# Two token parts in one 512-column matmul, added up afterwards, and other planned costs, in a two-block transformer kernel

## The chip, the cores and the metric

The kernel runs on one core of a Trainium2 chip. Its time is device microseconds, the median of 3 runs: 2299.26 us before (2298.84 to 2300.55). All times in this document are microseconds unless they are marked ns. Engine names are those of the profile: PE is TensorE's matmuls and PEld its weight loads, DVE is VectorE, ACT ScalarE, POOL GpSimd, SP SyncE, which issues most DMAs.

## What is computed

Two transformer blocks run one after the other on 256 tokens of width 2048, in float32. The part that the change touches is the end of the first block:

```python
mix = jnp.concatenate([a_out, b_out], axis=-1) @ w_out[l]       # 2048 x 2048
x = x + gt1 * mix
h2 = rms_norm(x, g_norm2[l]) * (1 + sc2) + sh2
ffn = (jax.nn.silu(h2 @ w_gate[l]) * (h2 @ w_up[l])) @ w_down[l]  # 2048 -> 5632 -> 2048
x = x + gt2 * ffn
```

Ahead of it come the modulation (`c_act @ w_ada`, which gives gt1, sc2, sh2, gt2 and others), the keys and values of a memory, the input projection, a differential attention (a_out) and a latent attention (b_out). Behind it the second block runs: an input projection with seven parts of 1024 columns and 6144 gate columns, a spatial gating branch, a state-space branch (a complex scan over the tokens), a cross-attention to the memory, gated sums of the three branches, an output projection and a norm.

## The kernel before

**Numbers in two parts.** Each float32 operand of a large matmul is split into hi (rounded to the format fp32r) and lo (what is left). A product is then three matmuls: hi weights by hi, hi weights by lo, lo weights by hi, all added in one PSUM accumulation. Activations lie transposed, 128 features of a k tile on the partitions and 256 tokens (T) as the columns; four k tiles share a unit of 1024 columns, and hi and lo have units of their own. `ws_tile` makes one output tile: it holds 128x128 blocks of the weights in the array and moves the 256 tokens past them, for 8 to 16 k tiles.

**Weights.** Halves of 512 KB (in the down projection 384 and 320 KB) come by DMA in an order that `build_items` lists. For each half ScalarE casts hi and VectorE subtracts lo (`prep_one`), some three halves ahead of their use. The modulation's weights (ada) come in the same stream; VectorE multiplies them by the condition and accumulates (`prep_ada(False)`), or TensorE does (`prep_ada(True)`), and a chunk ends with a fold on TensorE. Chunks 6 and 7 must be there before the feed-forward part starts (`until` in `ffn`).

**Order.** The instructions are put in order while the program is built, by a planner. It has one clock for each engine: `Engine` adds a planned cost for each instruction of VectorE (V), ScalarE (S) and GpSimd (P), `mm` adds one for each matmul (E). Work that follows a matmul is an event with a due time (`later`, `at`, `chain`). `tick`, called in the matmul loops (after every 8 k tiles, that is 24 matmuls, in the second block; after 4 k tiles of both gate and up in the feed-forward part; after 2 in the other tiles of the first block), runs the events that are due. `later(n, ...)` is due (n - 1) x TICK + 0.01 later, with TICK 2.6. Events that are not hot wait while a clock of V, S or P is more than LIMIT (6.0) ahead of E. `chain` runs stages one after the other, each due when the planned work of the last is done. A pair of ada pieces goes to VectorE while V is at most 4.0 ahead (ADA_LIMIT's last value); it goes to TensorE when four pieces have arrived and V is further ahead.

**The stages that the change touches.** The output projection makes 16 tiles from the differential attention (mixA, 8 k tiles each), then 16 from the latent attention (mixB); `add_gated` adds each to x with one VectorE instruction, and for mixB `split` goes on with hi, lo and the sum of squares of x. The feed-forward part runs in 4 chunks (FCH) of 11 hidden tiles (FT). For each hidden tile, gate and up are made side by side in two PSUM tiles, 16 k tiles each; `hidden` applies SiLU to the gate, multiplies by up and splits the result. The first two hidden tiles of the first chunk (`raw`) start before the norm is known and work on x itself. After the 11 hidden tiles come 16 tiles of the down projection with 11 k tiles each, again with `add_gated`.

**The second block's scan.** 32 pairs of state groups run beside the matmuls: `ssm_pair` starts a pair, and its stages turn, scan, back and out follow as a chain of which only turn is hot. The next pair comes SSM_EVERY (5) steps later, once stage back (for odd pairs out) of this one is planned. The branch's GLU matmul waits for the last pair (`until` "yg").

Of the kernel before, what the change touches and what calls it, by code (L numbers as in the profile page):

```python
# [236 lines left out]
class Half:  # L237
    def __init__(self, hi, lo):
        self.hi, self.lo = hi, lo


class Net:
# [429 lines left out]
    def xs_chunk(self, kind, n, X, nkt, done, group=2, k0=0, pre=None):  # L672

        ps = [self.ps(), self.ps()]
        for g in range(nkt // group):
# [3 lines left out]
            for j in range(group):  # L679
                k = g * group + j  # L680
                w_hi, w_lo = h.hi[:, n * j:n * (j + 1)], h.lo[:, n * j:n * (j + 1)]
                for b in range(2):
                    xh = self.kt(X[0], k0 + k)[:, P * b:P * (b + 1)]
                    xl = self.kt(X[1], k0 + k)[:, P * b:P * (b + 1)]
# [5 lines left out]
    def ws_tile(self, kind, X, sizes, off=0, ps=None):  # L690
# [14 lines left out]
        return ps[:, :T]  # L705
# [92 lines left out]
    def memory_kv(self, mem):  # L798
        nc = self.nc
        hi, lo = [], []  # L800
        for j in range(4):
            hi.append(self.u(F32R, "mh"))
            lo.append(self.u(F32R, "ml"))
            for k in range(4 * j, 4 * j + 4):
                self.hilo(self.kt(mem, k), self.kt(hi, k), self.kt(lo, k), self.par("memg", k))
# [10 lines left out]
        for m in range(8):  # L816
            ps = self.ws_tile("wk", (hi, lo), (8, 8))
# [13 lines left out]
        for c in range(2):  # L831
# [3 lines left out]
            self.xs_chunk("wv", 512, (hi, lo), 16, lambda ps, done=done: self.later(1, lambda: done(ps), True))  # L835
# [46 lines left out]
    def first_mod(self, X, half):  # L882
# [4 lines left out]
        hi, lo = self.H  # L887
        if half:
            hi[:2], lo[:2] = [None] * 2, [None] * 2
        for j in range(2):  # L890
            hi.append(self.u(F32R, "hh"))
            lo.append(self.u(F32R, "hl"))
        def pre(g):
            if g > 3:
                return
            ks = slice(T * (2 * g % 4), T * (2 * g % 4 + 2))
            u = 2 * half + g // 2
            for k in range(8 * half + 2 * g, 8 * half + 2 * g + 2):
                x = self.kt(X, k)
                nc.scalar.activation(x, x, AF.Identity, bias=self.modc(0, k), scale=self.A1[:, k:k + 1])  # L900
            nc.scalar.copy(hi[u][:, ks], X[u][:, ks])
# [1274 lines left out]
```

## Time and profile before

| what | value |
|---|---|
| median of 3 runs | 2299.26 us (2298.84 to 2300.55) |
| the profiled execution's own time | 2300.73 us |
| its span, first to last instruction | 2299.0 us |
| mean granted TensorE clock | 0.974 |
| PE busy | 2176.5 us (95%), 16384 matmuls |
| DVE busy | 1644.7 us (72%) |
| ACT busy | 995.6 us (43%) |
| POOL busy | 383.0 us (17%) |
| read from HBM | 498.10 MB, 224 GB/s over the span |

Busy time of a matmul is modelled from its start to its end, and matmuls overlap: one of 256 columns lasts some 284 ns in the profile, while the next starts earlier. So the pace is read from the starts in a timeline, or from the count of matmuls in a stretch. Stages by their first and last instructions: the front and the attentions until 446 us, the output projection from 446 to 564, the feed-forward part until 1348, the second block to the end.

### The profile page before, as it was taken

To read this page: it belongs to the slowest core of one execution; us is meant where nothing else is said; L and a number is where in the kernel's file an instruction comes from. 1 tells how busy PE (TensorE), PEld (TensorE's weight loads), DVE (VectorE), ACT (ScalarE), POOL (GpSimd) and SP (SyncE) were. 2 spreads that over 40 slices of the span, in tenths; PEclk is the share of its full clock that TensorE was granted. 3 is DMA by queue.
4 is the path that set the end of the run, shared out by engine and by line. 5 is a ranking of instruction groups with operands and counts; after the bars stand their busy time and mean duration, and the time that the engine had idled before them with its cause. 6 is when DMAs were issued, how large, how long until landed. Compare 5 with 4: busy or idle time off the path is not lost.

```text
span 2299.0 us, 41092 instructions
## 1 busy us (share of the span) xinstructions
PE 2176.5 (95%) x16384; PEld 2058.7 (90%) x16384; DVE 1644.7 (72%) x2339; ACT 995.6 (43%) x1533; POOL 383.0 (17%) x490
## 2 busy tenths in 40 slices
PE   6998898896899999999999999999899899989996
PEld 6776676696899999999999999899899899989996
DVE  7877798999884566754664565788787878765544
ACT  5454457534443333433434444443443434344442
POOL 3200325102000002954661040010000000000012
PEclk9999899898999999999999999999999999989998
DMA  9999777797795754855765585674666566545561
GB/s 380 318 343 347 286 235 246 256 346 292 256 322 152 235 179 131 262 195 176 229 233 180 165 295 182 230 247 160 205 199 204 173 199 205 189 156 179 188 213 37
DMA packets 159282, 518.65 MB, mean 226 GB/s; under 512 B 17481, under 2 KB 22473, under 8 KB 159089
## 3 DMA queue, kind: packets, MB, share of 16 engines
q1 hardware_dynamic: 150352, 498.97, 64.6%
q10 hardware_dynamic: 8736, 17.04, 2.0%
q8 instruction: 128, 2.10, 0.4%
q14 instruction: 66, 0.53, 0.1%
HBM read 498.10 MB, written 17.84 MB: 224 GB/s over the span
## 4 chain that ended last, share of the span: by engine, by line
PE 81%; DVE 10%; ACT 3%; issue 3%; DMA 2%; POOL 1%; ACTq 0%; SPq 0%; DVEq 0%; POOLq 0%
PE p L499 80%; DVE lo L210 3%; DVE ada L210 2%; ACT hi L210 2%; DVE s L210 1%; DMA raw<-in_w_ada 1%; PE p L709 1%; PE p L420 1%; POOL rt L210 1%; DVE om L210 1%; DVE yl L210 0%; DVE xl L210 0%; ACT p L210 0%; DMA raw<-in_wk 0%; DVE h L210 0%
## 5 line engine op out<-in xcount | busy, mean ns | idle before, releaser
L499 PE MATMUL p<-yh,hi 128*128 128x256 f32 x4544 | 1294.1, 285 | 9.2 <-ACT hi L210 5.3
L499 PE MATMUL p<-yl,hi 128*128 128x256 f32 x4544 | 1290.6, 284 | 12.0 <-DVE yl L210 12.0
L499 PE MATMUL p<-yh,lo 128*128 128x256 f32 x4544 | 1291.1, 284 | 4.4 <-DVE lo L210 4.3
L210 DVE TENSOR_TENSOR lo<-raw,hi 128x1024 fp32r<-128x1024 f32 (+2 forms) x740 | 883.8, 1214 | 335.5 <-ACT hi L210 329.0
L499 PEld LDWEIGHTS p<-yh,hi 128*128 128x128 f32 x4544 | 876.5, 193 | 19.5 <-issue 6.6
L499 PEld LDWEIGHTS p<-yl,hi 128*128 128x128 f32 x4544 | 876.4, 193 | 12.9 <-DVE yl L210 12.7
L499 PEld LDWEIGHTS p<-yh,lo 128*128 128x128 f32 x4544 | 876.5, 193 | 6.2 <-DVE lo L210 5.9
L210 ACT CAST hi<-raw 128x1024 fp32r<-128x1024 f32 (+2 forms) x740 | 709.2, 993 | 224.1 <-PE p L499 121.6
L210 POOL TENSOR_TENSOR acc<-acc,sq 128x256 f32<-128x256 f32 (+1 forms) x56 | 59.5, 1063 | 969.7 <-ACT sq L210 966.4
L210 DVE SCALAR_TENSOR_TENSOR ada<-raw,cact,ada 128x1024 f32<-128x1024 f32 x162 | 208.0, 1329 | 0.0
L499 PE MATMUL p<-hi,hh 128*128 128x512 f32 (+1 forms) x256 | 102.5, 401 | 8.4 <-ACT hh L210 6.6
L210 ACT ACTIVATE sg<-p 128x256 f32<-128x256 f32 x42 | 16.1, 383 | 216.9 <-PE p L499 216.9
L499 PE MATMUL p<-lo,hh 128*128 128x512 f32 (+1 forms) x256 | 101.3, 396 | 5.1 <-DVE lo L210 5.0
L210 DVE SCALAR_TENSOR_TENSOR x<-p,mod,x 128x256 f32<-128x256 f32 x96 | 46.2, 481 | 78.8 <-PE p L499 78.7
L499 PE MATMUL p<-hi,hl 128*128 128x512 f32 (+1 forms) x256 | 100.8, 394 | 0.0
L210 ACT ACTIVATE gt<-gt 128x256 f32<-128x256 f32 x48 | 20.1, 418 | 162.3 <-DVE gt L210 160.9
L210 POOL TENSOR_TENSOR rot<-tab,tab 128x256 f32<-128x256 f32 x64 | 63.9, 998 | 100.8 <-DMA dR<-rot 100.8
L499 PEld LDWEIGHTS p<-hi,hh 128*128 128x128 f32 x256 | 50.3, 197 | 22.2 <-ACT hh L210 7.0
L210 DVE TENSOR_TENSOR s<-p,rot 128x512 f32<-128x512 f32 x64 | 41.1, 685 | 36.6 <-PE p L499 36.5
L499 PEld LDWEIGHTS p<-lo,hh 128*128 128x128 f32 x256 | 50.2, 196 | 16.6 <-DVE lo L210 7.8
L210 POOL TENSOR_TENSOR rt<-rs 128x16 f32<-128x16 f32 (+2 forms) x26 | 13.5, 518 | 294.9 <-DVE rs L210 289.6
L210 POOL TENSOR_TENSOR rt<-tab,tab 128x256 f32<-128x256 f32 x64 | 62.2, 971 | 0.0
(300 smaller groups left out, 1972.4 us busy)
## 6 DMA issues: line engine op xcount, KB each, us to landing
raw<-in_w_ada SPq DMA_DIRECT2D x192, 512.0 KB
raw<-in_w_gu SPq DMA_DIRECT2D x176, 512.0 KB
raw<-in_w SPq DMA_DIRECT2D x96, 512.0 KB
raw<-in_w2g SPq DMA_DIRECT2D x96, 512.0 KB
raw<-in_w_out SPq DMA_DIRECT2D x64, 512.0 KB
raw<-in_w_in SPq DMA_DIRECT2D x56, 512.0 KB
raw<-in_w_down SPq DMA_DIRECT2D x64, 384.0 KB
raw<-in_wb SPq DMA_DIRECT2D x48, 512.0 KB
```

The source lines that it names most:

```text
L210: return f(*args, **kw)
L420: self.nc.tensor.matmul(self.ada_row[32 * j:32 * j + 32, :], left, w, start=start, stop=last)
L499: self.nc.tensor.matmul(out, lhsT, rhs, start=start, stop=stop)
L709: self.nc.tensor.transpose(out, in_, self.flip if flip else self.ident)
```

## The change

Activations now come in `Pairs`: hi and lo of a k tile lie side by side in 512 columns, two k tiles to a unit. In the output projection and in the feed-forward part (without its two early tiles) `mm_pair` runs one matmul of 512 columns with the hi weights, whose halves of the PSUM bank get the products with hi and with lo, and one of 256 columns with the lo weights into the first half. The two halves are added when they are read: `add_gated` runs twice, and `hidden` has a stage `fold` ahead of `gate`. The other stages use the new layout with the three matmuls of before. The planner's costs of VectorE, ScalarE, GpSimd and of a matmul are others.

```diff
 class Engine:
-    fixed = {"V": 0.07, "S": 0.2, "P": 0.06}
-    least = {"V": 0.2, "S": 0.23, "P": 0.28}
-    each = {"V": 0.00105, "S": 0.00074, "P": 0.00223}
+    fixed = {"V": 0.155, "S": 0.2, "P": 0.16}
+    least = {"V": 0.17, "S": 0.23, "P": 0.28}
+    each = {"V": 0.00106, "S": 0.00083, "P": 0.00223}
...
+class Pairs:
+    def __init__(self, net, name="y"):
+        self.net, self.name, self.units = net, name, []
+
+    def both(self, k):
+        while len(self.units) <= k // 2:
+            self.units.append(self.net.u(F32R, self.name))
+        return self.units[k // 2][:, 512 * (k % 2):512 * (k % 2 + 1)]
+
+    def hi(self, k):
+        return self.both(k)[:, :T]
+
+    def lo(self, k):
+        return self.both(k)[:, T:]
+
+    def two(self, k, part):
+        self.both(k)
+        return self.units[k // 2].rearrange("p (k h t) -> p k h t", k=2, h=2)[:, :, part]
...
     def mm(self, out, lhsT, rhs, start, stop):
         n = math.prod(rhs.shape[1:])
-        self.load.at["E"] += (max(n, 2 * P) if rhs.dtype == F32R else 4 * max(n, P)) / 2400
+        self.load.at["E"] += (max(n, P) + 32 if rhs.dtype == F32R else 4 * max(n, P)) / 2400
...
+    def mm_pair(self, ps, whi, wlo, X, k, start, stop, two):
+        if two:
+            self.mm(ps, whi, X.both(k), start, False)
+        else:
+            self.mm(ps[:, :T], whi, X.hi(k), start, False)
+            self.mm(ps[:, :T], whi, X.lo(k), False, False)
+        self.mm(ps[:, :T], wlo, X.hi(k), False, stop)
...
-    def ws_tile(self, kind, X, sizes, off=0, ps=None):
+    def ws_tile(self, kind, X, sizes, off=0, ps=None, two=False):
...
-                self.mm(ps[:, :T], h.hi[:, w], self.kt(X[0], off + k), k == 0, False)
-                self.mm(ps[:, :T], h.hi[:, w], self.kt(X[1], off + k), False, False)
-                self.mm(ps[:, :T], h.lo[:, w], self.kt(X[0], off + k), False, k == last)
+                self.mm_pair(ps, h.hi[:, w], h.lo[:, w], X, off + k, k == 0, k == last, two)
...
-            self.add_gated(self.ws_tile("w_out", self.mixA, (8,)), X, m, 2)
+            self.add_gated(self.ws_tile("w_out", self.mixA, (8,), two=True), X, m, 2)
...
-            self.add_gated(self.ws_tile("w_out", self.mixB, (8,)), X, m, 2, split)
+            self.add_gated(self.ws_tile("w_out", self.mixB, (8,), two=True), X, m, 2, split)
...
     def add_gated(self, ps, X, m, part, then=None):
         def add():
             x = self.kt(X, m)
-            self.nc.vector.scalar_tensor_tensor(x, ps, self.modc(part, m), x, op0=ALU.mult, op1=ALU.add)
+            for v in (ps[:, :T], ps[:, T:]):
+                self.nc.vector.scalar_tensor_tensor(x, v, self.modc(part, m), x, op0=ALU.mult, op1=ALU.add)
...
     def ffn(self):
...
                         for ps, hf in ((pg, hg), (pu, hu)):
+                            if not raw:
+                                self.mm_pair(ps, hf.hi[:, w], hf.lo[:, w], H, k, k == 0, k == 15, True)
+                                continue
...
-                self.add_gated(self.ws_tile("w_down", hid, (6, 5)), X, m, 5, split if last else None)
+                self.add_gated(self.ws_tile("w_down", hid, (6, 5), two=True), X, m, 5, split if last else None)
...
     def hidden(self, pg, pu, hid, j, raw):
+        def fold():
+            for v, ps in ((g, pg), (u, pu)):
+                nc.scalar.copy(v, ps[:, T:])
+                nc.vector.tensor_tensor(v, ps[:, :T], v, op=ALU.add)
+
         def gate():
-            if raw:
-                nc.scalar.activation(g, g, AF.Silu, bias=bias[0])
-            else:
-                nc.scalar.activation(g, pg[:, :T], AF.Silu)
+            nc.scalar.activation(g, g, AF.Silu, bias=bias[0] if raw else 0.0)
...
-                nc.vector.tensor_tensor(g, g, pu[:, :T], op=ALU.mult)
-            nc.scalar.copy(self.kt(hid[0], j), g)
+                nc.vector.tensor_tensor(g, g, u, op=ALU.mult)
+            nc.scalar.copy(hid.hi(j), g)
...
         elif j == FT - 1:
+            fold()
             gate()
             product()
             low()
         else:
-            self.chain(0, gate, product, low, hot=(gate, product, low))
+            self.chain(0, fold, gate, product, low, hot=(fold, gate, product, low))
```

Everywhere else `self.kt(X[0], k)` and `self.kt(X[1], k)` become `X.hi(k)` and `X.lo(k)`, and `grow` goes; copies of several k tiles at once (`first_mod`, `diff_norm`, the split of yg) write through `two`, with a stride of 512 columns.

## Rows read from the trace of the kernel before

**Rows 1.** The page: busy time (share of span), instructions; tenths in 40 slices.
```profile
PE 2176.5 (95%) x16384; PEld 2058.7 (90%) x16384; DVE 1644.7 (72%) x2339; ACT 995.6 (43%) x1533; POOL 383.0 (17%) x490
...
PE   6998898896899999999999999999899899989996
...
PEclk9999899898999999999999999999999999989998
```
**Rows 2.** Stretches: length, then busy us (count) by engine, granted clock, DMA share, GB/s.
```profile
446.00:500.00 54.00, 53.58 (x426) 51.50 (x427) 48.14 (x65) 24.52 (x35) 0.00 (x0) 1.00 0.91 317
500.00:564.00 64.00, 49.39 (x393) 48.53 (x391) 63.76 (x73) 22.89 (x43) 15.96 (x15) 0.91 0.87 319
613.00:1350.00 737.00, 736.53 (x6121) 735.50 (x6121) 449.93 (x622) 302.83 (x413) 219.69 (x259) 1.00 0.64 208
1410.00:2000.00 590.00, 575.72 (x4511) 553.04 (x4510) 474.07 (x748) 245.84 (x329) 5.93 (x11) 0.99 0.62 202
2000.00:2030.00 30.00, 21.44 (x140) 19.15 (x139) 21.45 (x35) 10.58 (x15) 0.00 (x0) 0.77 0.23 72
```
**Rows 3.** Timeline of PE, feed-forward part: start, duration, instruction; 15 starts apart.
```profile
1000.10 0.28 PE L499 MATMUL p<-yh,lo 128*128 128x256 f32 x1
...
1001.90 0.28 PE L499 MATMUL p<-yh,lo 128*128 128x256 f32 x1
```
**Rows 4.** Groups by form, 650 to 1400 us: busy, mean ns | idle before.
```profile
L499 PE MATMUL p<-yh,hi 128*128 128x256 f32 x2077 | 588.2, 283 | 0.0
...
L210 DVE TENSOR_TENSOR lo<-raw,hi 128x1024 fp32r<-128x1024 f32 x172 | 225.4, 1336 | 161.7 <-ACT hi L210 159.2 <-POOL cft L210 1.5 <-POOL rt L210 1.1
```
**Rows 5.** Waits of PE, 430 to 700 us: total, times, longest.
```profile
PE p L420 <- DVE ada L210: 12.0, 1, 12.0
```
**Rows 6.** Waits of PE, 1400 to 2300 us.
```profile
PE p L499 <- DVE yl L210: 12.0, 3, 6.6
PE p L499 <- DVE s L210: 6.3, 2, 4.7
PE p L499 <- ACT yh L210: 3.2, 1, 3.2
```
**Rows 7.** Timeline of PE in the second block, 512-column matmuls; 6 starts apart.
```profile
1471.16 0.39 PE L499 MATMUL p<-lo,yh 128*128 128x512 f32 x1
...
1472.52 0.39 PE L499 MATMUL p<-lo,yh 128*128 128x512 f32 x1
```
**Rows 8.** Instructions on tile mod: min/median/max ns, first and last start; here add_gated's.
```profile
L210 DVE SCALAR_TENSOR_TENSOR x<-p,mod,x x96: 471/484/486, 452.9 to 1348.2; 128x256 f32<-128x256 f32 x96
```
**Rows 9.** Timeline of DVE in the second half of the output projection.
```profile
510.01 0.47 DVE L210 SCALAR_TENSOR_TENSOR xl<-x,A,xh 128x256 fp32r<-128x256 f32 x1
510.41 0.47 DVE L210 SCALAR_TENSOR_TENSOR x<-p,mod,x 128x256 f32<-128x256 f32 x1
510.80 0.47 DVE L210 SCALAR_TENSOR_TENSOR xl<-x,A,xh 128x256 fp32r<-128x256 f32 x1
511.19 1.28 DVE L210 SCALAR_TENSOR_TENSOR ada<-raw,cact,ada 128x1024 f32<-128x1024 f32 x1
```
**Rows 10.** Instructions on tile sg of `hidden`: the gate and the product.
```profile
L210 ACT ACTIVATE sg<-p x42: 380/383/386, 620.5 to 1284.5; 128x256 f32<-128x256 f32 x42
L210 DVE TENSOR_TENSOR sg<-sg,p x42: 408/414/422, 627.3 to 1284.9; 128x256 f32<-128x256 f32 x42
```
**Rows 11.** Timeline at the last chunk's end: last gate, its lo, first down tile read.
```profile
1284.46 0.38 ACT L210 ACTIVATE sg<-p 128x256 f32<-128x256 f32 x1 [7.29 <-PE p L499]
...
1285.79 0.43 DVE L210 TENSOR_TENSOR yl<-sg,yh 128x256 fp32r<-128x256 f32 x1 [0.47 <-ACT yh L210]
...
1288.78 0.48 DVE L210 SCALAR_TENSOR_TENSOR x<-p,mod,x 128x256 f32<-128x256 f32 x1 [0.67 <-PE p L499]
```
**Rows 12.** Instructions on tile rdec: the scans, two for each of 32 pairs.
```profile
L210 DVE TENSOR_TENSOR_SCAN s<-rdec,sw x64: 664/676/689, 1440.1 to 2012.4; 128x256 f32<-128x256 f32 x64
```
**Rows 13.** Waits of PE, 0 to 430 us.
```profile
PE p L709 <- DVE km L210: 5.4, 1, 5.4
```

More of the change, by code (lines that the diff above doesn't have):

```diff
@@ L704, in ws_tile @@
                     self.tick()
-        return ps[:, :T]
+        return ps if two else ps[:, :T]
     def transpose(self, out, in_, flip=False):
@@ L886, in first_mod @@
         nc.vector.scalar_tensor_tensor(self.A1[:, ks], self.modc(1, 8 * half, 8), 1.0, self.par("g1", 8 * half, 8), op0=ALU.add, op1=ALU.mult)
-        hi, lo = self.H
+        H = self.H
         if half:
[L889 to L892, printed above, removed]
+            H.units[:4] = [None] * 4
         def pre(g):
@@ L895, in pre @@
                 return
-            ks = slice(T * (2 * g % 4), T * (2 * g % 4 + 2))
-            u = 2 * half + g // 2
-            for k in range(8 * half + 2 * g, 8 * half + 2 * g + 2):
+            k0 = 8 * half + 2 * g
+            xx = X[k0 // 4][:, T * (k0 % 4):T * (k0 % 4 + 2)].rearrange("p (k t) -> p k t", k=2)
+            for k in range(k0, k0 + 2):
                 x = self.kt(X, k)
                 nc.scalar.activation(x, x, AF.Identity, bias=self.modc(0, k), scale=self.A1[:, k:k + 1])
-            nc.scalar.copy(hi[u][:, ks], X[u][:, ks])
-            self.freer(512).tensor_tensor(lo[u][:, ks], X[u][:, ks], hi[u][:, ks].bitcast(F32), op=ALU.subtract)
+            nc.scalar.copy(H.two(k0, 0), xx)
+            self.freer(512).tensor_tensor(H.two(k0, 1), xx, H.two(k0, 0).bitcast(F32), op=ALU.subtract)
         pre(0)
@@ L908, in attention_block @@
         self.A1 = self.c([P, 16], s="A1")
-        self.H = H = ([], [])
+        self.H = H = Pairs(self, "hh")
         order = [[(ch, 0) if ch[0] == "c" else (ch[0], int(ch[1])) for ch in o] for o in ORDER]
@@ L1257, in diff_pv @@
         if h == 0:
-            self.mixA, self.otok = [[], []], []
+            self.mixA, self.otok = Pairs(self, "mixA"), []
         if h % 4 == 0:
-            self.grow(self.mixA)
             self.otok.append(self.u(s="ot"))
@@ L1428, in start_mla @@
     def start_mla(self):
-        self.mixB = [[], []]
+        self.mixB = Pairs(self, "mixB")
         self.later(MLA_AT, lambda: self.mla_next(0))
@@ L1461, in ffn @@
         nc = self.nc
-        X, H = self.X, ([], [])
+        X, H = self.X, Pairs(self, "h2")
         self.until(lambda: {6, 7} <= self.mod_done)
@@ L1472, in ffn @@
                 self.steps(self.ssm_early(), 2)
-            hid = ([], [])
+            hid = Pairs(self, "hid")
             for j in range(FT):
@@ L1747, in second @@
         yg_hl = self.yg_hl
-        Y = [[], []]
+        Y = Pairs(self, "yb")
         for m in range(8):
-            if m % 4 == 0:
-                self.grow(Y)
             ps = self.ws_tile("glu", yg_hl, (8,))
@@ L1769, in second @@
             self.chain(1, sigmoid, product, hi, lo, hot=(sigmoid, product, hi, lo))
-        M = [[], []]
-        for _ in range(4):
-            self.grow(M)
+        M = Pairs(self, "m")
         self.gate_loop(H, Y, third, "yb")
@@ L1812, in gated_tiles @@
     def gated_tiles(self, H, other, name):
-        Y = [[], []]
+        Y = Pairs(self, name)
         for m in range(8):
-            if m % 4 == 0:
-                self.grow(Y)
             self.gated(self.ws_tile("w2", H, (8, 8)), other(m), Y, m, name if m == 7 else None)
@@ L2123, in ssm_out @@
         t, bxt = self.t(s="ge")[:, :T], self.bxt
+        pair = lambda j: self.yg[j // 2][:, 512 * (j % 2):512 * (j % 2 + 1)].rearrange("p (k t) -> p k t", k=2)
         def skip():
@@ L2143, in hi @@
             self.cf = None
-            self.yg_hl = ([], [])
-            for j in range(2):
-                self.grow(self.yg_hl)
-                nc.scalar.copy(self.yg_hl[0][j], self.yg[j])
+            self.yg_hl = Pairs(self, "ygp")
+            for j in range(4):
+                nc.scalar.copy(self.yg_hl.two(2 * j, 0), pair(j))
         def lo():
-            for j in range(2):
-                self.freer(1024).tensor_tensor(self.yg_hl[1][j], self.yg[j], self.yg_hl[0][j].bitcast(F32), op=ALU.subtract)
+            for j in range(4):
+                h = self.yg_hl
+                self.freer(512).tensor_tensor(h.two(2 * j, 1), pair(j), h.two(2 * j, 0).bitcast(F32), op=ALU.subtract)
             self.ready_set.add("yg")
```

66 lines of the change are left out of this document (26 added, 40 removed).

## The prediction

> **What bounds the kernel now.** I read the page's totals and slices first, then stretches by stage, then the waits, then single instructions. TensorE is busy 95% of the span and its slices are nines nearly everywhere, with the granted clock at nine tenths or more in most [rows 1]. A busy TensorE is not yet one that sets the end, so the stretches decide [rows 2]. From 613 to 1350 us, the feed-forward part, 6121 matmuls start in 737 us: one each 120.4 ns, at a granted clock of 1.00. Single starts there lie 120 ns apart, 15 steps in 1.80 us [rows 3], and the costliest group has 0.0 us of idle time ahead of it [rows 4]. So this stage is pure matmul pace: what a matmul costs less there comes off the end. VectorE is busy 450 of those 737 us and ScalarE 303; both have room.
>
> Three other stretches are bound otherwise. From 500 to 564 us, the second half of the output projection, VectorE is busy 63.8 of 64 us [rows 2], and TensorE then stands 12.0 us for the last accumulation of the modulation (ada) [rows 5]. From 1410 to 2000 us TensorE leads again, with stalls that VectorE ends. From 2000 to 2030 only 140 matmuls start; at 120 ns they need 16.8 us, so 13.2 us go there, of which 6.3 and 3.2 us are waits for the tail of the state-space scan (s, yh) [rows 2, 6].
>
> **The change part by part.**
>
> *Pairs of matmuls become one.* Where two 256-column matmuls with the same hi weights follow each other (moving hi, then lo), one of 512 columns now runs; the third, lo weights by hi, stays. The kernel has 512-column matmuls of this kind in another place: they start 6 steps in 1.36 us apart, 227 ns [rows 7]. Two of 120 ns less one of 227 ns is 13 ns for each k tile. Their number, from the code: gate and up, 42 tiles (44 less the two early ones, which keep their form) x 16 k x 2 = 1344; down, 4 x 16 x 11 = 704; output projection, 32 x 8 = 256. The first two lie in the stretch that is pure pace: 2048 x 13 ns = 26.6 us. The 256 of the projection would give 3.3 us, but that stage ends with the wait of 12.0 us for VectorE, so I count them at nothing.
>
> The Trainium skill ("TensorE: Matmul & The Clock Gate", section "Back-to-back issue gap") speaks against this: it gives the gap as the columns over 2.4 GHz plus about 2.5 ns, so that a merged pair would save 2.5 ns alone. By that, 2048 pairs give 5.1 us (an estimate) and the sum below would be 2293. The rows differ: 120 ns against its 109 and 227 against its 216, so the fixed part here is about 13 ns, and I go by the rows.
>
> *The halves are added up afterwards.* add_gated now runs two scalar_tensor_tensors on VectorE instead of one, 96 more. One takes 484 ns [rows 8], but such instructions start 0.40 us apart when queued [rows 9]. In the down projection that is 64 x 0.40 = 25.6 us of VectorE. In the gate and up tiles fold adds, 42 times, two ScalarE copies out of PSUM (nearest row 383 ns) and two VectorE adds (nearest 414 ns) [rows 10]: 32 us of ScalarE and 35 of VectorE. With these VectorE has some 510 of 710 us and ScalarE 335; TensorE's matmuls cover all of it: nothing. Without the cover, at most the 25.6 + 35 us of VectorE would show. On the path fold could stand only at the end of a chunk, where the first down tile needs the 11th hidden tile at its last k. At 1284.46 us the last gate starts, at 1286.22 the lo part is there, and that down tile's result is read at 1288.78 [rows 11]. Its last three matmuls began some 0.5 us before that, so 2.0 us were to spare. fold puts one copy and one add ahead, 0.8 us, and 0.3 more as both engines take turns; the down tile itself is 0.13 us shorter. I take 0; if a weight cast or subtraction (1.34 us [rows 4]) stands in between at all four ends, at most 6 us.
>
> *The projection's stage on VectorE.* 32 of the additional instructions lie between 446 and 564 us. In the first 54 us VectorE has 5.9 us idle [rows 2], which takes up most of 16 x 0.40 = 6.4 us. In the second 64 us it has none, so 6.4 us come straight onto the wait that ends the stage: together +7. Against it, the build can give a pair of ada pieces to TensorE instead when its clock for VectorE is loaded, and with VectorE dearer in that clock it will do so sooner; one pair takes 2 x 1.28 us off VectorE [rows 9]. Bounds: -5 (five pairs moved) to +13 (no idle time used). I take +4, about one pair moved.
>
> *The build's clock.* Every instruction's planned cost changes, and with it the order in which the queues are filled; no instruction count follows directly. In the second part the planner looks at its events after each 24 matmuls. It charged 24 x 256 / 2400 = 2.56 us for them and now charges 24 x 288 / 2400 = 2.88, which is what they take by [rows 3]. A delay of "two steps" (2.61 us) so falls on the second look before and on the first now; the five steps between pairs of the state-space scan (10.41 us) fall on the fourth look in place of the fifth. The scans' 32 pairs now run from 1440.1 to about 2011.8 us (the pair's second scan starts at 2012.4 [rows 12]), 18.4 us or 6.4 looks each, so the chain within a pair also counts, not the delay alone. One look less would be 15.6 us a pair, half a look 17.0; anything under 18.0 moves the scan's end ahead of the place where TensorE now stands for it. The gain is bounded by 13.2 us there [rows 2] and the 12.0 us of waits for yl [rows 6]: -25. Denser scans also make VectorE fuller than 474 of 590 us, which could double those yl waits: +12. I take -5, half of the two waits on s and yh, since the planned costs of VectorE rise too. Ahead of 440 us nothing is merged; a reordered event there is worth about the longest wait of that kind, 5.4 us [rows 13], either way, and I take 0.
>
> *Layout.* hi and lo of a k tile now share a buffer; the units in use stay the same in number (6 for the hidden tiles, 8 for h2), and strided copies move the same elements: 0.
>
> **Sum**, on the profiled run's 2300.73 us (span 2299.0): -26.6 + 4 + 0 - 5 = 2273.1. The median is 1.5 us below that run, so 2272.
>
> **The rivals.**
>
> A. *The scan's tail vanishes* and the projection loses nothing: all 13.2 us at 2000 to 2030 and some of the yl waits come back. Time 2250 to 2262. For it: the delays fall on earlier looks. Against: 6.4 looks a pair say that the chain, not the delay, sets much of the pace.
>
> B. *Slower: the scan comes later.* The dearer VectorE (0.155 in place of 0.07 us fixed) makes the planner put off events that are not urgent while more than 6 us are queued, and three of the four stages of a scan pair are of that kind. TensorE already waits at the scan's end, so each 1 us more a pair is 31 us at the end. Without the 5 us of above, 22.6 us are left to outweigh, which takes 0.73 us a pair, 19.2 us in place of 18.4; at 1 us the time is 2273.1 + 5 + 31 - 1.5 = 2308. Against: the planner's TensorE is dearer too (12.5%), so VectorE's relative load rises only for short instructions.
>
> C. *The pair doesn't get cheaper.* The matmuls of [rows 7] are 512 columns after 512; alternating with 256 might keep the whole 13 ns. Bounds 0 to 13 ns a pair; at 0 the time is 2298. No row shows such an alternation at length; the weight loads beside the matmuls are the same kind, so I give it little.
>
> D. *The additions show*: projection at +13, chunk ends at +6, front +5: 2283 to 2296.
>
> **How the numbers follow.** Forecast (own range 2262 to 2283) 0.60; A 0.17; B 0.10; C 0.03; D 0.10. 0.2% of the median is 4.6 us, about what a measurement of this kernel can tell from no change, so faster is below 2294.7. Faster: 0.60 + 0.17 + 0.08 of D + 0.01 of C = 0.86; within: 0.02 of D, 0.02 of C and 0.01 of B = 0.05; slower 0.09 of B. The range 2252 to 2296 leaves out some 0.05 of A and 0.12 above.
>
> **What would show it.** In the feed-forward stretch a 512- and a 256-column matmul of one k tile should take 347 ns together in place of 360, and that stretch should be some 26 us shorter with no waits inside it; 360 would be C. Between the projection's start and the first gate tile the stage should be no shorter, with VectorE full and the wait for ada of 12 us or more. The scans' first and last start tell A and B apart: under 18.0 us a pair or over 19. A stall before each down projection would show fold on the path. The forecast is wrong if the feed-forward part's gain is there but given back behind 1400 us.

## The result, and the profile after

The changed kernel takes 2275.64 us (median of 4 runs, 2274.93 to 2277.15). The kernel before, on the same chip, takes 2299.91 (4 runs, 2298.84 to 2300.91). The ratio is 0.9895, with a 95% interval of 0.988 to 0.991. The forecast was 2272.0, 3.6 us below the result, in a range of 2252 to 2296.

The page of the changed kernel, the lines of [rows 1]: busy time and instructions by engine, then tenths in 40 slices.

```profile
PE 2150.8 (95%) x14128; PEld 1929.4 (85%) x14128; DVE 1711.9 (75%) x2510; ACT 1023.5 (45%) x1618; POOL 380.1 (17%) x490
...
PE   6998898996899999999999999999899899999996
...
PEclk9999999997999999999999999999999999999998
```

TensorE has 2256 matmuls fewer and 25.7 us less busy time, and the span is 24.9 us shorter (2274.1 against 2299.0). That the two times nearly agree is partly chance, as the stages show. Each mark below is the start of an instruction in the traces: the first matmul of the output projection, the first one on x itself (xh) in the early gate tile, the first one of the normed gate tiles, and the last addition of the down projection.

| us | projection starts | early gate (xh) | normed gate | last down addition | end |
|---|---|---|---|---|---|
| before | 446.4 | 570.6 | 599.3 | 1348.2 | 2299.0 |
| after | 426.4 | 567.7 | 594.9 | 1326.5 | 2274.1 |
| stage, before | | 124.2 | 28.7 | 748.9 | 950.8 |
| stage, after | | 141.3 | 27.2 | 731.6 | 947.6 |

The stretch ahead of the projection gives 20.0 us and the projection takes 17.1 of them back; the early tiles give 1.5, the feed-forward part 17.3 and the second block 3.2: 24.9 in all.

The stretches of the changed kernel that answer to [rows 2]: length, busy time and count by engine, granted clock, DMA share, GB/s.

```profile
426.00:480.00 54.00, 46.46 (x256) 36.70 (x255) 42.25 (x68) 19.97 (x36) 0.00 (x0) 0.97 0.74 257
480.00:540.00 60.00, 60.00 (x351) 49.69 (x350) 58.43 (x81) 26.87 (x43) 8.93 (x12) 1.00 0.85 299
540.00:564.00 24.00, 5.93 (x27) 1.89 (x26) 23.89 (x28) 5.50 (x9) 4.46 (x3) 0.60 0.99 391
613.00:1326.00 713.00, 712.95 (x4069) 621.34 (x4068) 509.04 (x762) 327.75 (x492) 224.36 (x258) 1.00 0.66 213
700.00:880.00 180.00, 180.00 (x1040) 158.72 (x1040) 133.32 (x281) 80.43 (x117) 55.12 (x78) 1.00 0.61 194
900.00:1320.00 420.00, 420.00 (x2379) 364.35 (x2378) 280.76 (x368) 193.02 (x292) 147.86 (x158) 1.00 0.65 206
1400.00:1980.00 580.00, 562.47 (x4398) 539.86 (x4398) 473.37 (x751) 241.42 (x322) 6.00 (x11) 0.99 0.64 202
1980.00:2010.00 30.00, 27.36 (x212) 26.22 (x212) 19.78 (x31) 15.15 (x23) 0.00 (x0) 0.94 0.39 129
```

The fifth and the sixth row are the reading that matters most. Both lie inside the feed-forward part, at a granted clock of 1.00 and with TensorE busy throughout, yet a k tile (two matmuls) takes 2 x 180 / 1040 = 346 ns in the one and 2 x 420 / 2379 = 353 ns in the other. The first three rows are the output projection: towards its end VectorE is nearly full (23.89 of 24 us), while TensorE is busy for only 5.93 of these 24 us, at a granted clock of 0.60. The last row shows that the hole behind the scans [rows 2, fifth row] is gone: 212 matmuls in 30 us in place of 140.

Single starts at the two paces, from the timeline of TensorE (start, duration, instruction):

```profile
800.13 0.39 PE L522 MATMUL p<-h,hi 128*128 128x512 f32 x1
800.36 0.28 PE L522 MATMUL p<-h,lo 128*128 128x256 f32 x1
800.48 0.39 PE L522 MATMUL p<-h,hi 128*128 128x512 f32 x1
...
1000.06 0.40 PE L522 MATMUL p<-h,hi 128*128 128x512 f32 x1
1000.29 0.28 PE L522 MATMUL p<-h,lo 128*128 128x256 f32 x1
1000.41 0.40 PE L522 MATMUL p<-h,hi 128*128 128x512 f32 x1
1000.64 0.28 PE L522 MATMUL p<-h,lo 128*128 128x256 f32 x1
1000.76 0.40 PE L522 MATMUL p<-h,hi 128*128 128x512 f32 x1
1001.00 0.28 PE L522 MATMUL p<-h,lo 128*128 128x256 f32 x1
1001.12 0.40 PE L522 MATMUL p<-h,hi 128*128 128x512 f32 x1
```

At 800 us the 512-column matmul holds the next one off for 230 ns each time. At 1000 us three k tiles take 350, 350 and 360 ns, 1.06 us in all, again and again. From the trace's starts the first pace is 346.7 ns a k tile (230.0 + 116.7) and the second 353.4 (236.5 + 116.9). The second begins at 893 us and holds for 1221 k tiles up to 1326 us.

What stands at the place where it begins:

```profile
893.04 0.39 PE L522 MATMUL p<-hid,hi 128*128 128x512 f32 x1
893.27 0.28 PE L522 MATMUL p<-hid,lo 128*128 128x256 f32 x1
893.60 0.50 PE L522 MATMUL p<-hid,hi 128*128 128x512 f32 x1
893.94 0.28 PE L522 MATMUL p<-hid,lo 128*128 128x256 f32 x1
```

From 893.27 the next start comes after 0.33 us in place of 0.12, and the one behind it after 0.34 in place of 0.23: the first down tile of the second chunk needs the eleventh hidden tile, whose lo part VectorE ends only at 893.54. This is the place that the forecast named for fold.

The waits of TensorE in the changed kernel, in the order 430 to 700 us, 640 to 1380 us, and 1400 us to the end (total, times, longest); they answer to [rows 5, 6]:

```profile
PE p L443 <- DVE ada L210: 18.8, 2, 18.1
PE p L522 <- ACT hi L210: 6.0, 1, 6.0
...
PE p L522 <- DVE diag L210: 2.0, 1, 2.0
PE p L522 <- POOL acc L210: 0.3, 1, 0.3
...
PE p L522 <- DVE yx L210: 6.1, 2, 5.4
PE p L522 <- DVE ya L210: 5.6, 1, 5.6
...
PE p L522 <- DVE sd L210: 2.2, 1, 2.2
...
PE p L522 <- ACT ygp L210: 2.1, 1, 2.1
```

The last of these views has no wait for s. The waits of 2.0 us for diag and of 0.3 us for acc stand at 1337 and 1329 us, behind the feed-forward part.

Fold and the additional additions run beside the matmuls, at about the durations that were taken for them. The instructions on the tiles mod, sg and rdec (count: minimum/median/maximum ns, first and last start) answer to [rows 8, 10, 12]; the last row are the scans of the second block.

```profile
L210 DVE SCALAR_TENSOR_TENSOR x<-p,mod,x x192: 470/484/489, 435.5 to 1326.5; 128x256 f32<-128x256 f32 x192
...
L210 ACT COPY sg<-p x84: 359/374/378, 616.3 to 1263.5; 128x256 f32<-128x256 f32 x84
L210 DVE TENSOR_TENSOR sg<-p,sg x84: 406/424/429, 619.8 to 1263.9; 128x256 f32<-128x256 f32 x84
...
L210 DVE TENSOR_TENSOR_SCAN s<-rdec,sw x64: 659/672/685, 1418.3 to 1980.9; 128x256 f32<-128x256 f32 x64
```

### The profile page after: what moved, and what is told of

Same layout as the page of the kernel before. It is cut to its first block, busy times and chain, and to the rows that moved or that the text cites. A ratio compares the mean times of both kernels' runs of the same rounds, so it can differ in the third digit from the quotient of the medians.

```text
span 2274.1 us, 36916 instructions
## 1 busy us (share of the span) xinstructions
PE 2150.8 (95%) x14128; PEld 1929.4 (85%) x14128; DVE 1711.9 (75%) x2510; ACT 1023.5 (45%) x1618; POOL 380.1 (17%) x490
## 4 chain that ended last, share of the span: by engine, by line
PE 72%; DVE 14%; DMA 4%; issue 3%; POOL 3%; ACT 2%; ACTq 0%; SPq 0%; DVEq 0%; POOLq 0%
PE p L522 72%; DVE lo L210 4%; DVE ada L210 3%; DVE s L210 2%; DMA raw<-in_w_ada 2%; ACT hi L210 1%; POOL tab L210 1%; POOL rt L210 1%; DVE lg L210 1%; POOL rot L210 1%; DVE om L210 1%; PE p L443 0%; POOL tabt L210 0%; DVE part L210 0%; DMA dV<-memV 0%
## 5 line engine op out<-in xcount | busy, mean ns | idle before, releaser
L522 PE MATMUL p<-h,hi 128*128 128x256 f32 (+1 forms) x4416 | 1031.2, 318 | 7.2 <-ACT hi L210 7.2
L522 PE MATMUL p<-h,lo 128*128 128x256 f32 x2880 | 812.7, 282 | 1.7 <-DVE lo L210 1.7
L522 PEld LDWEIGHTS p<-h,hi 128*128 128x128 f32 x4416 | 731.9, 191 | 74.7 <-ACT hi L210 8.6
L522 PEld LDWEIGHTS p<-h,lo 128*128 128x128 f32 x2880 | 549.5, 191 | 2.7 <-DVE lo L210 2.6
L522 PE MATMUL p<-hid,hi 128*128 128x512 f32 x704 | 247.8, 397 | 0.1
L522 PE MATMUL p<-hid,lo 128*128 128x256 f32 x704 | 197.6, 281 | 0.0
L522 PEld LDWEIGHTS p<-hid,hi 128*128 128x128 f32 x704 | 132.1, 188 | 32.3 <-DVE hid L210 0.4
L522 PEld LDWEIGHTS p<-hid,lo 128*128 128x128 f32 x704 | 133.0, 189 | 0.0
L522 PE MATMUL p<-m,hi 128*128 128x256 f32 x512 | 92.2, 283 | 0.0
L522 PEld LDWEIGHTS p<-m,hi 128*128 128x128 f32 x512 | 79.9, 192 | 0.0
```

## The experiments

Three questions were open. How is the time shared between the pairs of matmuls and the build's clock? Why does the projection give back what the stretch ahead of it gains? What sets the pace of the feed-forward stream? Ten kernels were run. Here is what each came to: the median and the ratio are those of all its runs, while the three columns behind them are read from the one execution that was profiled; "xh at" is the start of the early gate, and "stage" the feed-forward part from the normed gate to the last down addition.

| kernel | median us | ratio to before, 95% | xh at | stage | second block |
|---|---|---|---|---|---|
| after | 2275.64 | 0.9895 (0.988 to 0.991) | 567.7 | 731.6 | 947.6 |
| clock_only | 2287.61 | 0.9949 (0.9935 to 0.9964) | 560.0 | 750.1 | 948.0 |
| pairs_old_clock | 2280.24 | 0.9921 (0.9905 to 0.9938) | 579.0 | 723.8 | 948.4 |
| reset | 2277.72 | 0.9901 (0.9886 to 0.9916) | 568.2 | 730.1 | 950.0 |
| grouped | 2273.2 | 0.989 (0.9875 to 0.9904) | 566.2 | 729.1 | 947.2 |
| proj_single | 2268.43 | 0.9856 (0.9838 to 0.9873) | 559.7 | 732.8 | 946.8 |
| proj_single_grouped | 2267.37 | 0.9853 (0.9833 to 0.9872) | 561.4 | 729.6 | 946.7 |
| ada_half_dve | 2232.51, one run | | 527.9 | 729.1 | 946.6 |
| ada_half_dma | 2287.92, one run | | 577.9 | 733.9 | 946.5 |
| lo_first_one | 2270.07 | 0.9871 (0.9855 to 0.9888) | 560.2 | 733.0 | 949.1 |
| lo_first_all | 2273.67 | 0.9887 (0.9873 to 0.9902) | 559.3 | 734.4 | 948.5 |

**clock_only**: the kernel before with the changed planner's costs alone.

```diff
-    fixed = {"V": 0.07, "S": 0.2, "P": 0.06}
-    least = {"V": 0.2, "S": 0.23, "P": 0.28}
-    each = {"V": 0.00105, "S": 0.00074, "P": 0.00223}
+    fixed = {"V": 0.155, "S": 0.2, "P": 0.16}
+    least = {"V": 0.17, "S": 0.23, "P": 0.28}
+    each = {"V": 0.00106, "S": 0.00083, "P": 0.00223}
...
-        self.load.at["E"] += (max(n, 2 * P) if rhs.dtype == F32R else 4 * max(n, P)) / 2400
+        self.load.at["E"] += (max(n, P) + 32 if rhs.dtype == F32R else 4 * max(n, P)) / 2400
```

> The kernel before with the other planned costs alone (no pairs, no additions). Theory 1: the planned costs bring the first projection matmul forward by about 20 us (to 426), but the projection still ends when the ada pieces are through (the 160th piece is done at 564 us in both traces), so the first early gate tile starts at 568 +- 4 and the whole kernel gains only 3 to 7 us: 2293 to 2297. Rival 2: the 17 us that the projection lost are the 32 additional VectorE instructions; without them the early start is kept, the gate tile starts at 548 to 556 and the time is 2278 to 2286. Rival 3: the early start comes from the new layout, not from the costs: first projection matmul at 446, time 2297 to 2301.

Measured: 2287.61 us, 12 us below before, with the early gate at 560.0. Time and early gate both lie between the ranges of theory 1 and rival 2. So the new planned costs alone (the build's clock) bring the early gate 10.6 us forward.

**pairs_old_clock**: the changed kernel with those six values as before.

> The changed kernel with the planned costs of before (VectorE, ScalarE, GpSimd and matmul). Theory 1: the feed-forward part keeps its 18 to 27 us; the projection starts near 446 again and the early gate tile at 568 to 575, because the ada pieces set it; time 2274 to 2284. Rival 2: the 32 additions cost VectorE their full 12.8 us ahead of the gate tile, which starts at 580 to 585; time 2286 to 2290. In the second block the scan's pairs should take 18.4 us as before.

Measured: 2280.24 us, inside theory 1's time, with the early gate at 579.0, 8.4 us later than before and between the two ranges given. The feed-forward part shrinks by 25.1 us, close to the 26.6 of the forecast. With clock_only this gives a square: the pairs cost 8.4 us ahead of the early gate with the old costs and 7.7 with the new ones, and the new costs gain 10.6 us without the pairs and 11.3 with them. The stretches of pairs_old_clock:

```profile
700.00:880.00 180.00, 180.00 (x1041) 158.72 (x1040) 123.45 (x259) 81.04 (x119) 0.00 (x0) 1.00 0.59 191
...
900.00:1300.00 400.00, 400.00 (x2310) 352.69 (x2309) 284.96 (x362) 185.35 (x278) 214.59 (x249) 1.00 0.67 212
```

Both give 346 ns a k tile; from the starts, 1839 k tiles in a row keep 346.7 ns. The same code in the same loops thus runs nearly the whole part at the faster pace here, and 60% of it at the slower one in the changed kernel. This is the execution that was profiled, of 2278.18 us; the four runs are 2278.09, 2278.18, 2282.30 and 2282.37, and no trace shows which pace the two longer ones had.

**reset**: the changed kernel with seven transposes put into the stream, one ahead of the first gate tile of each later chunk and one ahead of the second down tile of each chunk.

```diff
+                if j == 0 and c:
+                    self.nc.tensor.transpose(pg[:, :P], self.ident, self.ident)
...
```

> The changed kernel with seven more PE transposes (of the identity, into a PSUM bank that the next matmul overwrites): ahead of the second down tile of each chunk and ahead of the first gate tile of chunks 2 to 4. In the changed kernel a k tile takes 346.7 ns until 893 us and 353.3 ns from there to 1326. Theory 1: which of the two it is, is settled by how the last interruption of the matmul stream left weight loads and matmuls to each other, and transposes leave the faster one (as at 427, 481 and 676 us); then all chunks run at 346.7, 1250 k tiles gain 6.7 ns, 8.3 us, less 7 x 0.2 us: time 2267 to 2270. Rival: the slower pace belongs to the buffers or the neighbours from chunk 2 on (GpSimd's tables, other weight buffers); then 353.3 stays and the time is 2275 to 2278.

Measured: 2277.72 us (2271.29 to 2278.41), in the rival's time, but the pace does not go by place as the rival said. From the starts: 346.7 ns behind the transposes at 712, 956, 1084 and 1141 us, 347.0 behind the one at 1267, and 353.3 behind those at 769 and 898. Behind a wait of 1.2 us at 1046 us it goes from 346.7 to 353.4. So a transpose is a place where the pace can change, but it doesn't restore the faster one; theory 1 falls in that form, and the rival with it.

**grouped**: gate's and up's 512-column matmuls first, then the two of 256 columns.

```diff
-                        for ps, hf in ((pg, hg), (pu, hu)):
-                            if not raw:
-                                self.mm_pair(ps, hf.hi[:, w], hf.lo[:, w], H, k, k == 0, k == 15, True)
-                                continue
+                        if not raw:
+                            for ps, hf in ((pg, hg), (pu, hu)):
+                                self.mm(ps, hf.hi[:, w], H.both(k), k == 0, False)
+                            for ps, hf in ((pg, hg), (pu, hu)):
+                                self.mm(ps[:, :T], hf.lo[:, w], H.hi(k), False, k == 15)
```

> The changed kernel with the order of the gate and up matmuls of one k turned from 512, 256, 512, 256 columns into 512, 512, 256, 256. Theory 1 (the slower pace belongs to the alternation after an interruption): a k of both takes 693 ns in all chunks, the 704 gate and up k tiles behind 893 us gain 6.7 ns, 4.7 us: time 2269 to 2273; the down tiles may still show 353.3. Rival: the pace belongs to the place in time: 707 ns per k of both from 893 us on, time 2275 to 2278. A third: two 512-column matmuls in a row have less cover for the weight loads, more than 707 ns: 2280 or more.

Measured: 2273.2 us, 0.2 above theory 1's range, and its interval overlaps that of the changed kernel. From the starts, the gate and up tiles of all four chunks keep one pace, 348.3 ns a k tile (696.6 for gate and up together, where theory 1 said 693, the rival 707 and the third over 707). The down tiles of the same execution, which still alternate, take 353.3 ns in the first chunk and 346.7 in the other three. So in this execution the two paces go with the alternation.

**proj_single**: the changed kernel with the output projection back to three 256-column matmuls and one addition.

```diff
-            self.add_gated(self.ws_tile("w_out", self.mixA, (8,), two=True), X, m, 2)
+            self.add_gated(self.ws_tile("w_out", self.mixA, (8,)), X, m, 2)
...
-            self.add_gated(self.ws_tile("w_out", self.mixB, (8,), two=True), X, m, 2, split)
+            self.add_gated(self.ws_tile("w_out", self.mixB, (8,)), X, m, 2, split)
...
-            for v in (ps[:, :T], ps[:, T:]):
+            for v in ((ps,) if part == 2 else (ps[:, :T], ps[:, T:])):
```

> The output projections back to three 256-column matmuls and one addition for each modulation of the second part; the feed-forward pairs and the build's clock stay. Theory 1 (the 32 more additions on a full VectorE are what the pairs cost ahead of the early gate: 7.7 us between clock_only's first early gate tile at 560.0 us and after's at 567.7): first early gate tile at 560 +-2 us, 2267 to 2270 us. Rival (the cost comes from the layout of the two halves or from where the modulation's matmuls land, not from the additions): first early gate tile at 566 to 570 us, 2274 to 2278 us.

Measured: 2268.43 us with the early gate at 559.7; theory 1 holds to the half microsecond. The stretch from the start up to the early gate, first of before, then of clock_only, of the changed kernel and of proj_single:

```profile
0.00:570.60 570.60, 496.66 (x2783) 409.02 (x2783) 481.28 (x620) 281.95 (x557) 120.43 (x194) 0.94 0.87 306
```
```profile
0.00:560.00 560.00, 491.25 (x2798) 406.20 (x2798) 485.06 (x629) 283.00 (x558) 114.53 (x184) 0.95 0.88 313
```
```profile
0.00:567.70 567.70, 492.55 (x2574) 391.90 (x2575) 490.59 (x656) 284.12 (x561) 111.75 (x184) 0.95 0.87 308
```
```profile
0.00:559.70 559.70, 488.04 (x2799) 404.02 (x2799) 485.28 (x630) 283.13 (x559) 114.31 (x184) 0.96 0.87 313
```

The third busy figure is VectorE's. Read as a ledger: the new planned costs leave VectorE 14.4 us less idle (570.6 - 481.3 = 89.3 to 560.0 - 485.1 = 74.9) and give it 3.8 us more work, so the early gate comes 10.6 us sooner. The pairs then add 5.5 us of work and 2.2 of idle time, 7.7 in all. Taking them out of the projection alone gives all of it back, though TensorE has 225 matmuls more ahead of the early gate. The edit takes out the merged matmuls and the additions together; since TensorE has more to do without the merging, the additions are the part that can cost.

**proj_single_grouped**: both edits together.

> The same edit of the output projections, with the feed-forward matmuls of gate and up in the order 512, 512, 256, 256. Theory 1: as in proj_single the first early gate tile comes at 558 to 562 us, the feed-forward part keeps the 729 us of grouped, 2262 to 2268 us. Rival (the projection's cost is not the additions): 2271 to 2276 us as grouped, first early gate tile at 565 to 569 us.

Measured: 2267.37 us, within theory 1's range, the early gate at 561.4 and the feed-forward part 729.6 us. Its interval and that of proj_single all but coincide, so the order of gate and up is worth nothing that these runs can tell. In its trace too gate and up take 348.3 ns a k tile, and the down tiles 346.7 in three chunks and 353.3 in the third. Both kernels lie below the changed one: the ends of their intervals (0.9873 and 0.9872) are under its lower end (0.988).

**ada_half_dve**: VectorE's accumulation of the modulation is left out for odd k, its planned cost and all transfers stay; so half of VectorE's part of the modulation's sum is missing.

```diff
+                elif k % 2:
+                    self.load.add("V", Engine.fixed["V"] + Engine.each["V"] * 1024)
                 else:
                     nc.vector.scalar_tensor_tensor(acc[n], w, c, acc[n], op0=ALU.mult, op1=ALU.add)
```

> VectorE's accumulation of the modulation for odd k is left out, so part of the modulation's sum is missing; the transfers stay. Theory 1 (VectorE, busy 525 of 564 us, ends the stretch up to the early gate): first early gate tile 30 us or more earlier than 567.7, at 500 to 538 us, and 2205 to 2245 us. Rival (the transfers of the modulation's weights, with a DMA share of 0.87, end it): first early gate tile at 560 to 568 us, 2267 to 2277 us.

**ada_half_dma**: only the first half of the columns of each ada piece is loaded, and used twice; VectorE works on it in two instructions of 512 columns.

```diff
-            self.nc.sync.dma_start(r[:, :n], src)
+            if isinstance(kind, tuple):
+                self.load.add("D", P * n * 4 / 358e3)
+                self.nc.sync.eng.dma_start(r[:, :512], src[:, :512])
+            else:
+                self.nc.sync.dma_start(r[:, :n], src)
...
-                    nc.vector.scalar_tensor_tensor(acc[n], w, c, acc[n], op0=ALU.mult, op1=ALU.add)
+                for o in (0, 512):
+                    y = acc[n][:, o:o + 512]
...
+                        v.scalar_tensor_tensor(y, w[:, :512], c, y, op0=ALU.mult, op1=ALU.add)
```

> Only the first half of the columns of each weight piece of the modulation is loaded and used twice, so the modulation is another one; VectorE's work stays. Theory 1 (VectorE ends the stretch up to the early gate): first early gate tile at 560 to 568 us, 2267 to 2277 us. Rival (the transfers end it): first early gate tile at 500 to 545 us, 2205 to 2255 us.

The stretch up to the early gate, first of ada_half_dve, then of ada_half_dma:

```profile
0.00:527.90 527.90, 479.07 (x2575) 384.48 (x2575) 410.76 (x590) 283.55 (x561) 102.01 (x184) 0.98 0.89 324
```
```profile
0.00:577.90 577.90, 498.54 (x2574) 396.64 (x2575) 506.85 (x792) 284.17 (x561) 104.83 (x184) 0.94 0.69 227
```

VectorE is busy 490.6 of the 567.7 us of this stretch in the changed kernel; the 525 of the expectation is a sum of durations that overlap. With 79.8 us less work on VectorE (490.6 to 410.8) the early gate comes 39.8 us sooner and the time falls to 2232.51, as theory 1 has it. With the DMA share down from 0.87 to 0.69 it comes no sooner at all: it comes 10.2 us later, beyond both ranges, and VectorE's work is 16.3 us more, because two instructions of 512 columns cost more than one of 1024. That side effect had been left out of the expectation. Both kernels, each from one run, agree that VectorE's work sets this stretch, not the transfers: of each microsecond of VectorE, half to two thirds reaches the early gate.

**lo_first_one** and **lo_first_all**: proj_single with the last k tile of a down tile turned round, its 256-column matmul first, in the first down tile of each chunk and in all down tiles. The low half of the last hidden tile is then needed later, and the wait that stands at 893 us in the changed kernel should go.

```diff
+        if two == "lo first" and stop:
+            self.mm(ps[:, :T], wlo, X.hi(k), start, False)
+            self.mm(ps, whi, X.both(k), False, True)
+            return
```

> proj_single with one change: in the first down tile of each chunk the eleventh (last) hidden tile's 256-column matmul goes ahead of its 512-column matmul, so that the low half of that hidden tile is needed some 117 ns later; the wait of about 0.1 us behind which after and proj_single went over to 353 ns for each k should go. Theory 1 (the pace of the stream is settled where it is interrupted, and this wait is the interruption): 346.7 ns for each k from about 670 us through 1300, the feed-forward part 8 us shorter than proj_single's 732.8 (724 to 726 us), 2258 to 2263 us. Rival (the pace changes there for another reason, or the swapped order interrupts the stream as well): 353 ns over half or more of the part, feed-forward part 730 to 735 us, 2265 to 2270 us.

> The same swap at the last k of all 128 down tiles, so that two 512-column matmuls follow on each other at each seam between down tiles. Theory 1 (only a wait settles the pace; a 512 behind a 512 does not): as lo_first_one, feed-forward part 724 to 727 us, 2258 to 2264 us. Rival (any change of the order settles it anew, so that both paces stand side by side by place): mean of 348 to 352 ns for each k, feed-forward part 727 to 732 us, 2262 to 2268 us.

Measured: lo_first_one 2270.07 us and lo_first_all 2273.67; nothing gained, and theory 1 falls in both. The wait did go, and the pace changed without it. The stretches of lo_first_one between its four turned tiles (at about 701, 888, 1072 and 1260 us; between the second and the third stretch stands a wait of 1.6 us):

```profile
705.00:885.00 180.00, 180.00 (x1021) 156.01 (x1020) 134.62 (x278) 78.20 (x112) 66.93 (x92) 1.00 0.60 193
890.00:1020.00 130.00, 130.00 (x752) 114.62 (x751) 97.86 (x110) 56.62 (x77) 124.61 (x129) 1.00 0.77 249
1075.00:1255.00 180.00, 180.00 (x1021) 155.98 (x1020) 105.57 (x144) 77.64 (x112) 0.00 (x0) 1.00 0.61 193
1262.00:1315.00 53.00, 53.00 (x307) 46.74 (x306) 42.69 (x71) 30.52 (x57) 9.70 (x13) 1.00 0.70 210
```

They are 353, 346, 353 and 345 ns a k tile. The first turned tile, in the timeline (x2: two matmuls drawn together):

```profile
700.68 0.39 PE L522 MATMUL p<-hid,hi 128*128 128x512 f32 x1
700.91 0.28 PE L522 MATMUL p<-hid,lo 128*128 128x256 f32 x1
701.03 0.39 PE L522 MATMUL p<-hid,hi 128*128 128x512 f32 x1
701.26 0.40 PE L522 MATMUL p<-hid,lo 128*128 128x256 f32 x2
701.50 0.63 PE L522 MATMUL p<-hid,hi 128*128 128x512 f32 x2
701.96 0.28 PE L522 MATMUL p<-hid,lo 128*128 128x256 f32 x1
```

No engine is waited for there, and ahead of it the k tiles take 346.7 ns, behind it 353. At 888 us the same turn does the reverse. In lo_first_all, with such a turn every 11 k tiles of the down projection, the faster pace holds up to the first turned k tile, at about 702 us, and hardly anywhere behind it; the mean is 352.1 ns. So lo_first_one fits the rival's broader sentence, that a change of the order settles the pace anew. In lo_first_all the two paces don't stand side by side, and its numbers lie above the rival's (348 to 352 ns, 727 to 732 us, 2262 to 2268 us): 352.1, 734.4 and 2273.67.

## Why the prediction was right, and where it was not

**Pairs in the feed-forward part: predicted -26.6, measured -17.3.** The mechanism is as forecast: the stage is pure matmul pace, and a k tile that took 360 ns [rows 3] takes less. The size was taken from one row of before, 227 ns for a 512-column matmul among its like [rows 7]. In the alternating stream there are two paces, 346.7 and 353.4 ns. Over the whole part the mean is 350.8, so 2048 x 9.2 ns = 18.8 us come off. The stage gives 1.5 us of it back: the wait for hi at its start is 6.0 us in place of 5.3, the slip at 893 us takes 0.3, and the rest was not traced. Only where the faster pace holds nearly throughout, in the traced execution of pairs_old_clock, does about the forecast's figure appear (-25.1). This is the mis-sized term: 1221 k tiles at 6.7 ns are 8.2 of the missing 9.3 us. Rival C asked whether the 13 ns survive the alternation and gave it 0.03; it was true in part: 9.2 of them survive on the mean.

The Trainium skill ("TensorE: Matmul & The Clock Gate", section "Back-to-back issue gap") gives the gap of an isolated matmul as the columns over 2.4 GHz plus about 2.5 ns, by which 5.1 us would have come off (an estimate). The Trainium skill says in the same section that in a stream of weight loads and matmuls both set the spacing, which the prediction left out. For this stream the runs decide against the formula: 9.2 ns a pair on the mean, 13.3 at the faster pace.

**The projection on VectorE: predicted +4, measured +7.7.** VectorE does end this stretch; ada_half_dve and ada_half_dma show it, and proj_single puts the cost down to the pairs in the projection, of which only the 32 additional additions add work. The working had a wrong part on each side. It let 5.9 us of VectorE's idle time take up additions, and idle time grew by 2.2 instead. It moved one pair of ada pieces to TensorE, and the planner moved five, one of them by the new costs alone (VectorE's instructions on ada ahead of the early gate: 146 before, 144 in clock_only, 136 in the changed kernel). And an addition seems to have cost nearer its whole 0.48 us than the 0.40 of a queued one: 32 x 0.48 less 4 x 2.56, for the four pairs that the additions moved, is 5.1 us, against 5.5 more of busy time in the ledger (with 0.40 it would be 2.6); with the idle time that is the 7.7. The wait for ada grew from 12.0 to 18.8 us, where the forecast had said 12 or more; clock_only has 17.8, so most of this growth comes from the earlier start of the projection.

**The front: predicted 0 (bounds -5.4 to +5.4), measured -10.6 by the clock alone.** This is the step that failed outright. I read it from one wait of TensorE there, 5.4 us for km [rows 13], and called it the longest of its kind. The view that it comes from has a longer one, 14.0 us:

```profile
PE p L499 <- ACT hi L210: 15.9, 3, 14.0
```

It ends at 14.0 us, at the kernel's very start, and is still there after the change (14.7 us), so it was no measure of the gain either. TensorE's waits do not bound this part; VectorE does, and clock_only leaves it 14.4 us less idle. Which of the planned costs does that, and by which reordered work, was not tested. The bound should have been VectorE's idle time ahead of the early gate, 89.3 us. The projection starts 20.0 us sooner, but what counts is when VectorE is through with the modulation, so only the net of front and projection shows: -10.6 + 7.7 = -2.9, against the +4 forecast. Of the two errors, 10.6 us one way and 3.7 the other, 6.9 us are left.

**Chunk ends: predicted 0, at most 6.** No wait longer than 0.3 us stands at any of them, so the additions and fold are hidden as said; VectorE is busy 509 of 713 us there and ScalarE 328, close to the 510 and 335 that were counted. One slip of some 0.3 us, at 893 us, is there all the same. I first took it for the cause of the slower pace behind it; lo_first_one took the slip away and got no time for it, so that theory fell.

**The clock in the second block: predicted -5, measured -3.2.** The scans begin 21.8 us earlier, as the end of the feed-forward part does, and run 18.13 us a pair in place of 18.44, neither under 18.0 (A) nor over 19 (B). Of [rows 6] only the waits for s (6.3 us) are gone. The others stand at the same places under new names, because the new layout names these tiles otherwise: the two longer waits for yl (4.7 and 6.6 us, at 1624 and 1830 us) are those for ya and yx (5.6 and 5.4, at 1610 and 1813), and that for yh (3.2) is that for ygp (2.1). New are 2.2 us for sd at 1413 us and the 2.3 us for diag and acc. That the new costs end the waits for s is borne out by both kernels: clock_only has none and 18.13 us a pair, pairs_old_clock has 6.4 us of them and 18.47. That they caused the 3.2 us is not: clock_only has 948.0 us there and pairs_old_clock, with the old costs, 948.4, 2.8 and 2.4 less than before, and the ten kernels spread from 946.5 to 950.0.

**The sum.** By stages, -17.3 for the feed-forward part in place of -26.6, -2.9 in place of +4 ahead of it, -1.5 for the early tiles where nothing was counted, -3.2 in place of -5. The forecast's total of -27.6 came within 2.7 us of the measured -24.9 because the errors of 9.3 and 6.9 us pulled against each other: the pairs work as forecast, but that the total came so near is luck. Rival D, the additions showing, was true in one of its three places, at 7.7 of its 13 us.

What stays open is which interruption leaves the stream at which pace. Both came behind transposes and behind a turned pair, and the same kernel's code met both. Nor do these traces tell whether one kernel has the same pace in every execution: each pace is read from one, and the four runs of reset spread over 7.1 us and those of proj_single_grouped over 9.6, while those of clock_only, without pairs, spread over 0.9. A pattern that holds the faster pace by construction was not found; the order 512, 512, 256, 256 held 348.3 ns in every gate and up tile of its two traces.

## What to carry to other kernels

Merge matmuls where TensorE alone sets the pace, and not where the engine that must add up the halves is the one that ends the stage: the same merge gave 17 us in the feed-forward part and cost 8 in the projection, and leaving it out there made the fastest kernels here (2268.43 and 2267.37 us). Bound a reordering by the idle time of the engine that ends the stretch, not by the waits of the busiest one. Before multiplying a per-instruction gain by 2048, look for the longest run of the very pattern, and keep the spread of its pace as the range. When waits are compared before and after, go by their place and not by the tile's name alone, which the change may have altered.

## What the runs showed of the hardware that was not expected

An alternating stream of 512- and 256-column matmuls, each with its own weights, at a granted clock of 1.00 and with no wait, ran at one of two steady paces: 346.7 ns for the two, or a cycle of 350, 350 and 360 ns. It kept the one it had for hundreds of microseconds (1839 k tiles at the faster, 1221 at the slower), and each change that was followed up stood where the alternation is broken: by a wait, by another instruction, or by two matmuls of the same width in a row. Not every such break changed the pace. Why one break leads to the one pace and the next to the other was not settled. Two other patterns showed one pace: the pure 256-column stream of before 120 ns a matmul, and the order 512, 512, 256, 256 696.6 ns for the four.

A VectorE accumulation on 1024 columns takes 1.28 us [rows 9]. Cut in two halves of 512, its share of the stretch grew by some 16 us over 136 pieces, about 0.12 us a piece.
